# Rebuilt stage boundaries, another order in the RWKV core, and split operands in the mLSTM heads of a three-block network

## The chip, the cores and the metric

The program runs on one core of a Trainium2 chip. The core has five engines with a queue each: TensorE (PE; matmul, with its weight loads listed apart as PEld), VectorE (DVE), ScalarE (ACT), GpSimd (POOL), and SyncE (SP), which issues the DMAs. The metric is the device time of one execution in microseconds (us), lower is better. Times are medians over runs; the trace comes from one profiled execution.

## The reference

One sequence of 512 tokens, width 1024, float32 throughout, goes through three blocks, one layer each in the parts named here:

```python
# block 1: conv branch + sparse attention, merged; gelu FFN (2816) with a 3-tap conv; gated extra input; rmsnorm
# block 2: hyena mixer + FFN, then an RWKV-7 mixer (16 heads of 64, both directions) + FFN, rmsnorm
def step(state, inp):                      # RWKV-7, once forward and once backward, 512 steps
    sa = jnp.einsum('bhvk,bhk->bhv', state, kk_t)
    state = state * w_t[:, :, None, :] - sa[..., None] * (kk_t * a_t)[:, :, None, :] + v_t[..., None] * k_t[:, :, None, :]
    return state, jnp.einsum('bhvk,bhk->bhv', state, r_t)
# block 3: mLSTM (4 heads of 512) and HGRN2 (8 heads of 128) side by side, gated sum,
#          layernorm(ALPHA * x + mixed @ w_out), silu FFN, layernorm
w = jnp.exp(log_w - m_t[..., None]) * jnp.einsum('bhtd,bhsd->bhts', qc, kc)     # mLSTM
num, den = jnp.einsum('bhts,bhsd->bhtd', w, vc), jnp.sum(w, axis=-1)            # + carried state
h = num / jnp.maximum(jnp.abs(den), jnp.exp(-m_t))[..., None]
```

## The kernel before

Activations lie with channels on the 128 partitions and the 512 tokens along the free axis: eight tiles `x[0..7]` of 128x512. A dense layer (`dense`, `dense_steps`) takes chunks of 256 output channels. A chunk's weights arrive as `wraw` (1 MB by one DMA from SP); ACT rounds them to `wh` (line 156, reduced-precision fp32r), DVE takes the rest as `wl` (line 157), and the activations are split in the same way into `h` and `l`. `mm3` then adds `h*wh + l*wh + h*wl` in PSUM, three fp32r matmuls in place of one f32 matmul. A plain f32 matmul shows as two records in the trace. Where a sum over channels is wanted, a f32 matmul with a matrix of ones (`spread`) puts it on all partitions; POOL adds up the tiles before it (`sqa`, `lna`).

A scheduler orders the instructions of each engine from the dependencies, except where `manual_schedule` keeps the written order on the engines named. PE is in written order in the attention, the hyena mixer, the RWKV core and HGRN.

*RWKV core* (`core`, 1600 to 2257 us): eight pairs of heads go through a pipeline of stages written as Python generators, one step per `next`. In period p: `C` runs the recurrence over eight 64-token chunks of pair p-1 (three steps each: `R` is copied out of PSUM by DVE, `ch<-R,WT` follows, the new values `SV` are written by DVE for one head and by ACT for the other, then `ch<-SV,bkT`); `A`, `T`, `B` prepare pair p (`A`: gram products `pa/pb<-AX,bk`, which DVE multiplies by masks into `GB` (line 1419) and ACT copies into `AX` (line 1421); `T`: transposes `pb<-csts,bk` (line 1441); `B`: inverse of a triangular matrix, whose small part is solved on DVE row by row (`tw`, `W`) and comes back through DRAM and ACT as `wd`); `L`, `E` and `D` prepare pair p+1; `Y` ends pair p-2; `F` is one step of filling dense work (`pf<-x,wf`). `PLACES` gives each step a place, `ORDER` sorts them, and `FIRST` is the order of period 0:

```python
ORDER = [n for _, n in sorted((x, n) for n, v in PLACES.items() for x in v)]
for p in range(9):
    ...
    for n in ORDER if p else FIRST:
        if n in G:
            next(G[n], 0)
```

Only PE's order is fixed so; DVE, ACT and POOL are ordered by the scheduler.

*mLSTM* (`mlstm`, 2625 to 3092 us): per head, dense q, k, v and output gate, a lower-triangular weight matrix `pt` in four row blocks of 512, 384, 256 and 128 columns, and f32 matmuls of `pt` with ones (`pd`, the denominator) and with `v` (`po`), of constant rows (`rows`), and of two sums over channels. *HGRN* (`hgrn`, to 3345 us) weaves two heads and a stream of dense work step by step (`weave`). *LayerNorm* (class of that name, twice in block 3) sums six tiles, takes a preliminary mean off every tile (`center`), sums the squares (`lnq`, `lna`), corrects by the leftover mean `dm` (five tiles on DVE, three on POOL, line 1777), and scales and biases (lines 1782, 1783).

Of the kernel before, what the change touches and what calls it, by code (L numbers as in the profile page):

```python
# [83 lines left out]
class K:  # L84
# [179 lines left out]
    def begin(s):  # L264

        x, w = [], None
# [952 lines left out]
def key_norms(s, pairs, q, rid, ps, w):  # L1219
# [42 lines left out]
def core(s, ep, hw, ha, hg, xmd, xd):  # L1262
# [278 lines left out]
    def stage_c(p):  # L1541
# [6 lines left out]
        for i in range(8):  # L1548
# [16 lines left out]
            nc.scalar.activation(SV[HX[1], :, i, 1], q[HX[1], 1], AF.Copy, scale=-1.0)  # L1565
# [110 lines left out]
    def run(rp, pp):  # L1676
        env.rp, env.pp = rp, pp
        with s.tc.manual_schedule(engines={mybir.EngineType.PE}):
# [47 lines left out]
TAIL = 64  # L1726

# [677 lines left out]
```

## Time and profile before

| | us |
|---|---|
| time, median of 3 runs (lowest to highest) | 4038.02 (4033.47 to 4039.93) |
| the profiled execution: time | 4039.87 |
| the profiled execution: span in the trace | 4038.1 |
| busy PE / DVE / ACT / POOL | 3805.7 / 2391.3 / 1609.4 / 721.8 |
| mean granted TensorE clock | 0.967 |

The span runs from the first to the last instruction of the trace; 1.8 us of the execution lie around it. Busy times of different engines overlap. The granted clock is a share of 2.4 GHz; a stretch at 0.50 runs at 1.2 GHz.

### The profile page before, as it was taken

The page shows a single profiled execution, that of the slowest core. Times are in us where ns is not written, and L with a number is a line of the kernel's source. Part 1 is how long each engine was busy: PE and PEld are TensorE (multiplying, and loading weights), DVE is VectorE, ACT ScalarE, POOL GpSimd, SP SyncE. Part 2 cuts the span into 40 slices and gives each one's busy share as a digit, 9 for nine tenths or more (in the row PEclk, how much of TensorE's full clock was granted, in tenths as well). Part 3 has the DMA queues.
Part 4 walks back from the last instruction along what each step waited for, and adds up shares of the span by engine and source line. Part 5 has one row for each costly group of instructions (what it writes and reads, how often), then busy time and mean ns, then how long its engine had stood idle before and what let it go on. Part 6 is the DMA issues. An engine that isn't in the chain of part 4 may idle for free.

```text
span 4038.1 us, 51960 instructions
## 1 busy us (share of the span) xinstructions
PE 3805.7 (94%) x20982; PEld 2972.4 (74%) x20982; DVE 2391.3 (59%) x3492; ACT 1609.4 (40%) x2182; POOL 721.8 (18%) x574
## 2 busy tenths in 40 slices
PE   8899999999899998899878899999999999998998
PEld 6556888777788884666656688877777888877886
DVE  5965665677866556476675655465554644554334
ACT  3455433464443333344432433355553332333222
POOL 1000200032620006444442100101111000030001
PEclk9899999999999999999888999999999999999999
DMA  5122223222232324544433223132223212431221
GB/s 214 49 77 95 104 80 114 91 94 94 86 124 82 112 81 154 149 113 122 115 98 103 94 89 105 58 145 84 86 97 114 94 71 79 138 123 71 99 88 64
DMA packets 184132, 408.69 MB, mean 101 GB/s; under 512 B 80361, under 2 KB 98314, under 8 KB 155988
## 3 DMA queue, kind: packets, MB, share of 16 engines
q1 hardware_dynamic: 183892, 405.38, 30.3%
q8 instruction: 165, 2.70, 0.3%
q14 instruction: 75, 0.61, 0.0%
HBM read 364.37 MB, written 43.57 MB: 101 GB/s over the span
## 4 chain that ended last, share of the span: by engine, by line
PE 55%; DVE 9%; ACT 3%; DMA 2%; issue 2%; POOL 1%; SPq 0%; DVEq 0%; POOLq 0%; ACTq 0%
PE pacc L138 47%; PE pf L138 3%; PE pb L138 2%; PE ch L138 1%; PE pa L138 1%; DVE ct L1929 1%; DVE wl L157 1%; DVE tw L1471 1%; DVE GB L1419 1%; DVE W L1473 1%; PE py L138 1%; DMA x<-rid 0%; DVE xr L1151 0%; ACT wh L156 0%; DMA Lr<-dn 0%
## 5 line engine op out<-in xcount | busy, mean ns | idle before, releaser
L138 PE MATMUL pacc<-h,wh 128*128 128x512 f32 x3792 | 1499.7, 398 | 33.2 <-ACT wh L156 19.1
L138 PE MATMUL pacc<-l,wh 128*128 128x512 f32 x3792 | 1487.3, 392 | 1.2 <-DVE l L188 1.2
L138 PE MATMUL pacc<-h,wl 128*128 128x512 f32 x3792 | 1484.8, 393 | 3.8 <-DVE wl L157 3.8
L138 PEld LDWEIGHTS pacc<-h,wh 128*128 128x128 f32 x3792 | 718.7, 190 | 213.9 <-issue 30.8
L138 PEld LDWEIGHTS pacc<-h,wl 128*128 128x128 f32 x3792 | 716.8, 189 | 163.2 <-DVE wl L157 8.2
L138 PEld LDWEIGHTS pacc<-l,wh 128*128 128x128 f32 x3792 | 718.0, 189 | 151.7 <-issue 3.9
L157 DVE TENSOR_TENSOR wl<-wraw,wh 128x2048 fp32r<-128x2048 f32 (+2 forms) x276 | 611.4, 2215 | 368.2 <-ACT wh L156 368.0
L156 ACT ACTIVATE wh<-wraw 128x2048 fp32r<-128x2048 f32 (+2 forms) x276 | 492.8, 1785 | 790.3 <-PE pacc L138 694.0
L138 PE MATMUL pf<-x,wf 128*128 128x256 f32 x736 | 217.3, 418 | 5.6 <-DMA x<-yd 3.3
L223 POOL TENSOR_TENSOR sqa<-sq 128x512 f32<-128x512 f32 x12 | 19.3, 1608 | 1006.5 <-ACT sq L218 666.6
L138 PEld LDWEIGHTS pf<-x,wf 128*128 128x128 f32 x736 | 130.9, 197 | 39.5 <-issue 10.5
L295 DVE TENSOR_TENSOR z<-pacc,rstd 128x512 f32<-128x512 f32 x132 | 90.3, 691 | 101.5 <-PE pacc L138 101.2
L323 DVE TENSOR_TENSOR x<-pacc,x 128x512 f32<-128x512 f32 x48 | 33.1, 691 | 178.3 <-PE pacc L138 178.3
L223 POOL TENSOR_TENSOR sqa<-sqa,sq 128x512 f32<-128x512 f32 x50 | 100.3, 2006 | 109.3 <-ACT sq L218 101.2
L309 ACT ACTIVATE ct<-ct 128x512 f32<-128x512 f32 x66 | 41.8, 634 | 180.9 <-DVE ct L306 120.5
L138 PE MATMUL pacc<-wh,h 128*128 128x512 f32 (+2 forms) x288 | 103.6, 363 | 9.6 <-DVE z L983 9.6
L1836 POOL TENSOR_TENSOR x<-x,z 128x512 f32<-128x512 f32 x16 | 22.8, 1446 | 456.4 <-DVE z L1835 456.4
L138 PE MATMUL pacc<-wl,h 128*128 128x512 f32 (+2 forms) x288 | 103.4, 359 | 0.4 <-DVE wl L157 0.4
L138 PE MATMUL pacc<-wh,l 128*128 128x512 f32 (+2 forms) x288 | 103.1, 361 | 0.0
L290 DVE TENSOR_TENSOR hv<-ct,pacc 128x512 f32<-128x512 f32 x22 | 15.1, 688 | 143.6 <-PE pacc L138 143.6
L552 DVE SCALAR_TENSOR_TENSOR x<-sg,vecs,x 128x491 f32<-128x491 f32 (+28 forms) x120 | 86.2, 743 | 5.5 <-ACT x L543 5.0
L1422 POOL TENSOR_TENSOR AX<-AX,rwc 64x512 f32<-64x512 f32 x64 | 81.9, 1279 | 33.2 <-ACT AX L1421 29.6
(521 smaller groups left out, 4982.0 us busy)
## 6 DMA issues: line engine op xcount, KB each, us to landing
wraw<-in_w_up_dram SPq DMA_DIRECT2D x44, 1024.0 KB, 4.8
wraw<-in_w_down_dram SPq DMA_DIRECT2D x32, 704.0 KB, 4.0
wraw<-in_w_up2a_dram SPq DMA_DIRECT2D x22, 1024.0 KB, 4.8
wraw<-in_w_up2b_dram SPq DMA_DIRECT2D x22, 1024.0 KB, 4.8
x<-xmd SPq DMA_DIRECT2D x72, 256.0 KB, 2.7
wraw<-in_w1a_dram SPq DMA_DIRECT2D x16, 1024.0 KB, 4.8
wraw<-in_w3q_dram SPq DMA_DIRECT2D x16, 1024.0 KB, 4.9
wraw<-in_hy_w_in_dram SPq DMA_DIRECT2D x12, 1024.0 KB, 4.7
```

What stands on the lines that cost most here:

```text
L138: s.nc.tensor.matmul(out, a, b, start=start, stop=stop)
L156: s.nc.scalar.activation(wh[:, :n], raw[:, :n], AF.Copy)
L157: s.nc.vector.tensor_tensor(wl[:, :n], raw[:, :n], wh[:, :n].bitcast(F), op=SUB)
L223: nc.gpsimd.tensor_tensor(a2, acc, q, op=ADD)
L295: nc.vector.tensor_tensor(z, ps, rstd, op=MUL)
L309: nc.scalar.activation(t, t, act)
L552: nc.vector.scalar_tensor_tensor(y[:, d:], u[:, :T - d], w, y[:, d:], op0=MUL, op1=ADD)
L1419: nc.vector.tensor_tensor(GB[h, hs], q[h], mask[h, None].to_broadcast([64, 4, 2, 64]), op=MUL)
L1422: nc.gpsimd.tensor_tensor(AX[o, hs, X], AX[o, hs, X], mask[o, None].to_broadcast([64, 4, 2, 64]), op=MUL)
L1471: nc.vector.tensor_tensor(tw[:, 0:i, 0:i], W[:, 0:i, 0:i].rearrange("p j c -> p c j"), L[:, 0:i, i][:, None, :].to_broadcast([P, i, i]), o ...
L1473: nc.vector.tensor_reduce(W[:, i, 0:i], tw[:, 0:i, 0:i], axis=AX.X, op=ADD, negate=True)
L1929: nc.vector.scalar_tensor_tensor(t[:, d:], z[:, :T - d], w[3 - d], t[:, d:], op0=MUL, op1=ADD)
```

## The change

Three groups of edits are made together. At stage boundaries: `begin` loads `x` and the first weights in an interleaved order and splits those weights in four parts; a dummy activation (`ready`) loads ACT's table ahead of a norm; `phase(weights_last=True)` places the weight pool behind the activation pool in SBUF for the RWKV block's FFN and for block 3; the last `w_o` tile of the core lies in a `GB` buffer; LayerNorm's sums, shifts and scaling come in another order, written out by hand on PE, DVE and ACT, and its last step writes the split `h` and `l` directly; HGRN's sum of squares is made earlier and its matmul steps later. In the core: the `SV` copy of the second head goes from ACT to DVE, and `PLACES` and `FIRST` have other numbers. In the mLSTM heads: the f32 matmuls with `pt`, `v`, ones and rows become two or three fp32r matmuls with operands split by ACT and DVE (the block of 128 columns stays f32).

```diff
+    def parts(s, src):
+        h, l = (s.ap.tile([P, T], R, name="sp", tag="nrm", bufs=4) for _ in range(2))
+        s.nc.scalar.activation(h, src, AF.Copy)
+        s.nc.vector.tensor_tensor(l, src, h.bitcast(F), op=SUB)
+        return h, l
+    def mm2(s, out, w, hl, start, stop):
+        s.mm(out, w, hl[0], start, False)
+        s.mm(out, w, hl[1], False, stop)
+    def spread2(s, acc, onesr):
+        p = s.ms()
+        s.mm2(p, onesr, s.parts(acc), True, True)
+        return p
+    def ready(s, x):
+        t = s.ap.tile([P, 128], F, name="rdy", tag="rdy", bufs=1)[:, 0:1]
+        s.nc.scalar.activation(t, x[:, 0:1], AF.Abs_reciprocal_sqrt, scale=0.0, bias=s.eps(1.0))
     def sumsq_soon(s, xs):
         acc = s.sumsq_of(xs[:-1])
+        s.ready(xs[-2])
...
     def begin(s):
-        for n in range(NT):
-            if n == 2:
-                w = s.wsplit("w1a", 0, 8, 256)
-            x.append(s.xtile())
-            s.nc.sync.dma_start(x[n], s.I["xT"][n])
+        nc.scalar.activation(t, s.ones[:, 0:1], AF.Copy)
+        for i in range(4):
+            a = slice(512 * i, 512 * i + 512)
+            nc.sync.dma_start(x[2 * i], s.I["xT"][2 * i])
+            nc.sync.dma_start(raw[:, a], s.I["w1a"][0][:, a])
+            nc.sync.dma_start(x[2 * i + 1], s.I["xT"][2 * i + 1])
+            nc.scalar.activation(wh[:, a], raw[:, a], AF.Copy)
+            nc.vector.tensor_tensor(wl[:, a], raw[:, a], wh[:, a].bitcast(F), op=SUB)
...
 PLACES = {
-    "A": [1.21, 5.84, 5.85, 8.154, 8.47],
-    "T": [9.2, 10.47, 11.63, 11.63, 11.76, 11.76],
...
+    "A": [1.21, 5.84, 5.977, 6.971, 6.971],
+    "T": [10.229, 10.229, 10.402, 10.8, 11.732, 12.877],
...
             nc.vector.tensor_scalar(SV[HX[0], :, i, 0], q[HX[0], 1], -1.0, None, op0=MUL)
-            nc.scalar.activation(SV[HX[1], :, i, 1], q[HX[1], 1], AF.Copy, scale=-1.0)
+            nc.vector.tensor_scalar(SV[HX[1], :, i, 1], q[HX[1], 1], -1.0, None, op0=MUL)
...
-    def finish(s, g, b):
+    def finish(s, g, b, split=False):
...
         nc.scalar.activation(dm, s.p1, AF.Copy, scale=1.0 / 1024)
         nc.scalar.activation(w, s.p1, AF.Square, scale=1.0 / 1024)
+        for n in (4, 5, 6, 7, 0, 1):
+            shift(n)
+        nc.vector.scalar_tensor_tensor(w, s.p2, 1.0 / 1024, w, op0=MUL, op1=SUB)
+        nc.scalar.activation(r, w, AF.Abs_reciprocal_sqrt, bias=k.eps(1e-5))
+        nc.vector.tensor_scalar(v, w, 1.0, 1e-5, op0=MUL, op1=ADD)
+        shift(2)
...
             nc.vector.scalar_tensor_tensor(x, x, k.v(g, n), r, op0=MUL, op1=MUL)
+            if split:
+                out.append([k.ap.tile([P, T], R, name=i, tag="xs", bufs=16) for i in "hl"])
+                nc.scalar.activation(out[n][0], x, AF.Identity, bias=k.v(b, n))
+                if n:
+                    low(n - 1)
...
-        for c in range(4):
-            for i, _ in enumerate(s.dense_steps("w_out3", c, 8, 256, ms, evac_x, 2 * c)):
-                if (c, i) == (3, 2):
+        wo = s.wsplit("w_out3", 3, 8, 256)
+        w = s.wsplit("w_up3", 0, 8, 256)
+        with tc.manual_schedule(engines=MANUAL):
+            for i, _ in enumerate(s.dense_steps("w_out3", 3, 8, 256, ms, evac_x, 6, w=wo)):
+                if i == 2:
                     ln.mean()
-        ln.late(6)
-        ln.late(7)
-        ln.early()
-        ln.finish("ln1_g", "ln1_b")
+            s.ready(x[7])
+            ln.late(6)
+            ln.early()
+            ln.late(7)
+            xs = ln.finish("ln1_g", "ln1_b", split=True)
...
-    for si in range(4):
-        s.mm(pd[:, si * P:], s.ones, pt[:, off[si]:off[si] + T - si * P], si == 0, si == 3)
+    for si in range(3):
+        s.mm2(pd[:, si * P:], onesr, ps[si], si == 0, False)
+    s.mm(pd[:, 3 * P:], s.ones, pt[:, off[3]:], False, True)
...
-        for si in range(4):
-            s.mm(po[:, si * P:], v[:, si, j * P:(j + 1) * P], pt[:, off[si]:off[si] + T - si * P], si == 0, si == 3)
+        for si in range(3):
+            s.mm3(po[:, si * P:], vs[si][0][:, c], vs[si][1][:, c], *ps[si], si == 0, False)
+        s.mm(po[:, 3 * P:], v[:, c], pt[:, off[3]:], False, True)
...
-        yield
-        r = s.rstd_of(s.sumsq([o]), 1.0 / 128, 1e-6)
+        sq = s.sumsq_of([o])
+        yield
+        yield
+        yield
+        r = s.rstd_of(s.spread(sq), 1.0 / 128, 1e-6)
...
-            weave((head(2 * j), 22), (head(2 * j + 1), 22), (fill, (24, 40, 24, TAIL)[j]))
+            weave((head(2 * j), 24), (head(2 * j + 1), 24), (fill, (24, 40, 24, TAIL)[j]))
```

The order tables move instructions in rows, of which three places follow. Line numbers grow by 5 to 37 from before to after (1419 is 1456, 1349 is 1386, 1564 and 1565 are 1601 and 1602, 138 is 143).

On DVE, in the core's period 2 of the kernel before, around the masks of the second `A` pair (`GB`; the first line is the normalised key `x` of the next pair, which needs `rid`, a row of norms that comes back from DRAM):

```order
L1349 SCALAR_TENSOR_TENSOR x_13085<-x_13083,vecs_63,x_13085 128x512 [waits DMAHW5_49,DMAHW7_49,DMAHW3_49,DMAHW0_49]
L1419 TENSOR_TENSOR GB_13035<-pa_13036,rwc_10884 64x512 [waits PE_49]
L1419 TENSOR_TENSOR GB_13035<-pa_13037,rwc_10884 64x512 [waits PE_49]
L1419 TENSOR_TENSOR GB_13035<-pb_13052,rwc_10884 64x512 [waits PE_49]
L1419 TENSOR_TENSOR GB_13035<-pb_13053,rwc_10884 64x512 [waits PE_49]
L1555 COPY R_13076<-ch_13071 128x128 [waits PE_49]
L1564 TENSOR_SCALAR SV_12411<-ch_13071 64x2x64 [waits DVE_49,PE_49]
L1368 SCALAR_TENSOR_TENSOR e65_13367<-w65_13364,rwc_10884 128x520 [waits Activation_49]
```

And the same place in the changed kernel, from the third of the four masks on:

```order
L1456 TENSOR_TENSOR GB_13019<-pb_13036,rwc_10895 64x512 [waits PE_49]
L1456 TENSOR_TENSOR GB_13019<-pb_13037,rwc_10895 64x512 [waits PE_49]
L1601 TENSOR_SCALAR SV_12426<-ch_13006 64x2x64 [waits PE_49]
L1602 TENSOR_SCALAR SV_12426<-ch_13006 64x2x64
L1272 COPY fn_12825<-pa_13061 16x128 [waits PE_49]
L1612 TENSOR_TENSOR z1_13074<-ch_13006,Z_12960 128x128 [waits PE_49,Pool_49]
L1613 TENSOR_TENSOR SV_12426<-z1_13074,pcs_11770 64x2x64 [waits DVE_49]
L1614 TENSOR_TENSOR SV_12426<-z1_13074,pcs_11770 64x2x64
L1592 COPY R_13091<-ch_13086 128x128 [waits PE_49]
L1386 SCALAR_TENSOR_TENSOR x_13100<-x_13098,vecs_63,x_13100 128x512 [waits DMAHW6_49,DMAHW2_49,DMAHW0_49]
L1601 TENSOR_SCALAR SV_12426<-ch_13086 64x2x64 [waits DVE_49,PE_49]
L1602 TENSOR_SCALAR SV_12426<-ch_13086 64x2x64 [waits DVE_49]
```

The key that waits for a DMA stood ahead of the four masks, and now stands behind them, behind the new values `SV` of that chunk and behind the next `R`, directly ahead of the next two `SV`.

On PE, in period 2 before, from the second `A` pair to the first `T` (`pf` is a step of `F`; `ch` and `py` belong to `C`):

```order
L138 MATMUL pa<-AX,bk 128x128 x8
L138 MATMUL pb<-AX,bk 128x128 x8
L138 MATMUL pf<-x,wf 128x256
L138 MATMUL ch<-SV,AX 64x64 x4
L138 MATMUL py<-AX,SV 64x64 x4
L138 MATMUL pf<-x,wf 128x256
L1441 MATMUL pb<-csts,bk 128x64 x8
```

In the changed kernel the same stretch is longer; the piece begins behind the first `F` that follows the second `A` pair:

```order
L143 MATMUL ch<-R,WT 64x64 x4
L1270 MATMUL pa<-csts,fn 16x128
L143 MATMUL pf<-x,wf 128x256
L143 MATMUL ch<-SV,bkT 64x64 x4
L143 MATMUL py<-GB,SV 64x64 x4
L143 MATMUL pf<-x,wf 128x256 x2
L143 MATMUL ch<-SV,AX 64x64 x4
L143 MATMUL py<-AX,SV 64x64 x4
L143 MATMUL pf<-x,wf 128x256 x2
L143 MATMUL ch<-R,WT 64x64 x4
L143 MATMUL pf<-x,wf 128x256
L1478 MATMUL pb<-csts,bk 128x64 x16
```

Between the second `A` pair and the first `T` stood one step of `C` and two of `F`; now stand there four steps of `C`, seven of `F` and the row with `fn`.

On PE, at the first LayerNorm, the sums with the matrix of ones before (`x` are the last two tiles, `lnq` their squares, `lna` the sum of the other six squares):

```order
L138 MATMUL pacc_27002<-x_26756,ones_66 128x512 [waits DVE_49]
L138 MATMUL pacc_27002<-x_26758,ones_66 128x512 [waits DVE_49]
L138 MATMUL pacc_27003<-lnq_27036,ones_66 128x512 [waits Activation_49]
L138 MATMUL pacc_27003<-lnq_27040,ones_66 128x512 [waits Activation_49]
L138 MATMUL pacc_27003<-lna_27000,ones_66 128x512 [waits Pool_49]
```

and after:

```order
L143 MATMUL pacc_27300<-x_27046,ones_66 128x512 [waits DVE_49]
L143 MATMUL pacc_27301<-lnq_27334,ones_66 128x512 [waits Activation_49]
L143 MATMUL pacc_27301<-lna_27298,ones_66 128x512 [waits Pool_49]
L143 MATMUL pacc_27300<-x_27048,ones_66 128x512 [waits DVE_49]
L143 MATMUL pacc_27301<-lnq_27338,ones_66 128x512 [waits Activation_49]
L143 MATMUL pacc_27423<-h_27370,wh_27242 128x512 [waits Activation_49]
```

The sum of the six squares stood last and stands third; each tile's square follows its own tile; the last row is the first matmul of the FFN.

## Rows read from the trace of the kernel before

**Rows 1.** The page, first part: busy us, share of the span, instructions.

```profile
PE 3805.7 (94%) x20982; PEld 2972.4 (74%) x20982; DVE 2391.3 (59%) x3492; ACT 1609.4 (40%) x2182; POOL 721.8 (18%) x574
```

**Rows 2.** Windows by stage: us, busy of each engine, then PEclk, DMA share.

```profile
25.00:345.00 320.00, 292.75 (x1368) 198.47 (x1367) 229.00 (x534) 158.33 (x266) 19.50 (x15) 0.95 0.26 91
...
1690.00:1977.00 287.00, 263.24 (x3345) 188.92 (x3340) 194.19 (x433) 120.78 (x252) 133.51 (x142) 0.92 0.43 115
...
2625.00:3092.00 467.00, 462.05 (x1988) 360.28 (x1989) 259.17 (x281) 237.88 (x291) 63.11 (x51) 0.99 0.28 100
...
3620.00:3660.00 40.00, 21.66 (x52) 12.76 (x51) 31.62 (x36) 21.61 (x32) 14.68 (x8) 0.70 0.11 40
```

**Rows 3.** PE's waits in the core, 1600 to 2257 us: total, times, longest.

```profile
PE pa L138 <- DVE t L1382: 18.9, 7, 5.5
...
PE pb L1441 <- ACT AX L1421: 15.5, 5, 4.5
...
PE ch L138 <- DVE R L1555: 12.6, 17, 3.6
...
PE ch L138 <- ACT SV L1565: 7.2, 11, 1.3
...
PE pb L138 <- ACT wd L1498: 6.5, 2, 6.1
```

**Rows 4.** Windows at half clock, after a wait in the core and in HGRN.

```profile
1788.05:1798.25 10.20, 9.96 (x50) 6.21 (x50) 5.63 (x17) 5.55 (x9) 5.97 (x8) 0.50 0.40 80
...
3272.80:3276.30 3.50, 3.50 (x10) 2.70 (x9) 3.35 (x6) 2.60 (x3) 0.00 (x0) 0.51 0.16 62
```

**Rows 5.** Timeline of the start, ACT and POOL: start, us, what, idle before.

```profile
10.09 1.91 ACT L156 ACTIVATE wh<-wraw 128x2048 fp32r<-128x2048 f32 x1 [2.44 <-DMA wraw<-in_w1a_dram]
...
13.28 10.69 POOL L223 TENSOR_TENSOR sqa<-sqa,sq 128x512 f32<-128x512 f32 x6 [4.90 <-ACT sq L218]
```

**Rows 6.** Timeline of the core, DVE and PE.

```profile
1784.11 1.47 DVE L1349 SCALAR_TENSOR_TENSOR x<-x,vecs 128x512 f32<-128x512 f32 x1 [0.84 <-DMA x<-rid]
...
1785.50 1.40 DVE L1419 TENSOR_TENSOR GB<-pa,rwc 64x512 f32<-64x512 f32 x2
...
1788.29 1.11 PE L1441 MATMUL pb<-csts,bk 64*128 64x64 f32 x8 [2.23 <-ACT AX L1421]
...
1685.13 1.22 PE L138 MATMUL pa<-t,rwc 128*128 128x512 f32 x1 [5.52 <-DVE t L1382]
```

**Rows 7.** Groups by line, ACT in the core: busy, mean ns, idle before.

```profile
L1565 ACT ACTIVATE SV<-ch 64x128 f32<-64x128 f32 x64 | 17.4, 272 | 170.3 <-DVE SV L1564 170.1
```

**Rows 8.** Timeline of PE in the mLSTM stage, head 0.

```profile
2702.04 0.39 PE L138 MATMUL pacc<-wh,h 128*128 128x512 f32 x1
...
2702.27 0.39 PE L138 MATMUL pacc<-wl,h 128*128 128x512 f32 x1
...
2736.03 2.32 PE L138 MATMUL pacc<-pt,ones 128*128 128x512 f32 x8
...
2738.27 1.12 PE L138 MATMUL pacc<-rows,c 4*128 4x512 f32 x2
...
2739.32 8.90 PE L138 MATMUL pacc<-pt,v 128*128 128x512 f32 x32
```

**Rows 9.** PE's waits in the HGRN stage, 3092 to 3345 us.

```profile
PE pacc L138 <- ACT sq L218: 5.9, 3, 2.0
```

**Rows 10.** Timeline of the first LayerNorm, DVE, ACT and PE.

```profile
3636.48 6.30 DVE L1777 TENSOR_TENSOR x<-x,z 128x512 f32<-128x512 f32 x5 [2.80 <-ACT z L1774]
...
3647.08 1.38 ACT L1783 ACTIVATE x<-x,vecs 128x512 f32<-128x512 f32 x2 [2.27 <-DVE x L1782]
...
3649.03 1.22 PE L138 MATMUL pacc<-h,wh 128*128 128x512 f32 x2 [9.46 <-ACT h L187]
```

**Rows 11.** Timeline at the norm ahead of the RWKV mixer, ACT and PE.

```profile
1529.38 1.28 ACT L197 ACT_TABLE_LOAD   x1
...
1529.68 1.02 PE L138 MATMUL pacc<-sq,ones 128*128 128x512 f32 x2
```

More of the change, by code (lines that the diff above doesn't have):

```diff
@@ L1726 @@
 TAIL = 64
+MANUAL = {mybir.EngineType.PE, mybir.EngineType.DVE, mybir.EngineType.Activation}
 class LayerNorm:
@@ L1765, in late, with shift @@
         s.k.mm(s.p1, s.k.ones, s.x[n], n == 6, n == 7)
-        s.k.mm(s.p2, s.k.ones, s.last.pop(n), n == 6, False)
+        s.k.mm(s.p2, s.k.ones, s.last.pop(n), n == 6, n == 7)
     def early(s):
-        s.k.mm(s.p2, s.k.ones, s.q, False, True)
-    def finish(s, g, b):
+        s.k.mm(s.p2, s.k.ones, s.q, False, False)
+    def finish(s, g, b, split=False):
         k, nc = s.k, s.k.nc
-        dm, w = k.tmp("z"), k.tmp("ct")
+        dm, w, v, u = k.tmp("z"), k.tmp("ct"), k.tmp("ct"), k.tmp("ct")
+        r = k.ap.tile([P, T], F, name="rstd", tag="rstd", bufs=2)
+        def shift(n):
+            (nc.vector if n < 4 else nc.gpsimd).tensor_tensor(s.x[n], s.x[n], dm, op=SUB)
@@ L1786, in block3 @@
+        if split:
+            low(7)
+            for n, x in enumerate(s.x):
+                nc.scalar.activation(x, x, AF.Identity, bias=k.v(b, n))
+        return out
 def block3(s, x):
@@ L1797, in block3 @@
         ccol, rows = gates(s, x, bp)
+        onesr = bp.tile([P, P], R, name="onesr")
+        nc.scalar.activation(onesr, s.ones, AF.Copy)
+        selr = bp.tile([36, T], R, name="selr")
+        for a in (slice(0, 4), slice(32, 36)):
+            nc.scalar.activation(selr[a], cst[a, 0:T], AF.Copy)
+        cst = cst, onesr, selr
         for h in range(4):
-            mlstm(s, bp, h, xs, ccol, rows, cst, hA)
+            mlstm(s, bp, h, xs, ccol, rows, cst, hA, None if h else w)
     with tc.tile_pool(name="b3h", bufs=1) as bp:
@@ L1874, in during @@
                 ln.late(6)
-        s.ffn(x, xs, None, "w_up3", "w_down3", AF.Silu, update=upd, during=during)
+        s.ffn(x, xs, None, "w_up3", "w_down3", AF.Silu, update=upd, during=during, w=w)
+    with tc.manual_schedule(engines=MANUAL):
+        s.ready(x[7])
+        ln.early()
         ln.late(7)
-        ln.early()
-    ln.finish("ln2_g", "ln2_b")
+        ln.finish("ln2_g", "ln2_b")
     return x
@@ L1911, in gates, with mlstm, row @@
     nc.vector.tensor_copy(ccol, q)
-    return ccol, (mt, rows[32:36])
-def mlstm(s, bp, h, xs, ccol, rows, cst, hA):
+    hl = [bp.tile([36, T], R, name="rows" + i) for i in "hl"]
+    for a in (slice(0, 4), slice(32, 36)):
+        nc.scalar.activation(hl[0][a], rows[a], AF.Copy)
+        nc.vector.tensor_tensor(hl[1][a], rows[a], hl[0][a].bitcast(F), op=SUB)
+    return ccol, hl
+def mlstm(s, bp, h, xs, ccol, rows, cst, hA, w0):
     nc, I = s.nc, s.I
-    sel = cst[0:4, h * P:(h + 1) * P], cst[32:36, h * P:(h + 1) * P]
+    cst, onesr, selr = cst
     mneg = cst[:, 512:640]
+    def row(a):
+        p = s.ms()
+        a = slice(32 * a, 32 * a + 4)
+        s.mm2(p, selr[a, h * P:(h + 1) * P], [r[a] for r in rows], True, True)
+        return p
     qk = {}
@@ L1933, in mlstm @@
     for c in range(4):
-        s.dense("w3q", 4 * h + c, 8, 256, xs, evac_qk, 2 * c)
-    pn = s.ms()
-    s.mm(pn, sel[0], rows[0])
+        s.dense("w3q", 4 * h + c, 8, 256, xs, evac_qk, 2 * c, w=None if c else w0)
+    pn = row(0)
     nm = s.tmp("z")
@@ L2004, in mlstm @@
         acc = a
-    pm = s.ms()
-    s.mm(pm, s.ones, acc)
+    pm = s.spread2(acc, onesr)
     mu = s.tmp("z")
@@ L2381, in body @@
         x = block2b(s, x)
-        with s.phase():
+        with s.phase(weights_last=True):
             x = block3(s, x)
```

88 lines of the change are left out of this document (55 added, 33 removed), and 16 rows, old and new, of the table PLACES.

## The prediction

> **What bounds the kernel now.** I read the busy shares first: PE is busy 94% of the span, no other engine above 59% [rows 1]. So a stage either streams matmuls, and only fewer or cheaper matmuls shorten it, or PE waits, and then the wait that ends last counts. The windows by stage tell the two apart [rows 2]: the mLSTM stage has PE busy 462 of 467 us (matmuls bound it), the RWKV core from 1690 to 1977 us has 263 of 287 at a clock of 0.92, the first LayerNorm boundary 22 of 40 at 0.70, the attention 293 of 320. Then the waits of the two worst places were followed to what releases them.
>
> In the core PE's waits go to four causes of 7 us and more [rows 3]. The clock makes them dearer: behind the wait that ends at 1788.29 PE works 10.2 us at 0.50, half of 2.4 GHz, though it is busy 9.96 of them [rows 4]. The rule I take from these rows: behind a wait of some 2 us comes a stretch at half clock, and where PE is busy in it, half of it is lost. At 0.92 over 287 us, 0.08 x 287 / 0.5 = 46 us of the four full periods are at half clock.
>
> **The start.** Before, the first weights (1 MB in one piece) are rounded at 10.09, after ACT idled 2.44 us for that DMA, and POOL's chain of squares pauses 4.90 us, because ACT is at the weights when it should square the third tile [rows 5]. That chain sets the end of the first norm (13.28 + 10.69 = 23.97). With the weights in quarters and the table loaded early, squares come one after another, and the pause goes: -4.7 us. Bounds: -3 if ACT's four small roundings stay in its way, -6 if the load before the first tile counts too.
>
> **The core.** DVE runs strictly in order in this trace: at 1784.11 it stands 0.84 us for the DMA of `rid`, computes the key 1.47 us, and only then masks the second `A` pair into `GB` (four of 0.70 us). ACT's copy `AX` follows, and PE's first `T`, which needs that PSUM buffer, waits 2.23 us [rows 6]. Five such waits make 15.5 us [rows 3]. In the new order the key stands behind the masks, and seven `F` and four `C` lie between `A` and `T`, against four masks of 2.8 us in all. So the 15.5 us should go. Of the 46 us at half clock I give these waits 32 (four others, of 3.5 as behind HGRN's wait [rows 4], belong to `pa<-t,rwc`); half of it is lost, and a little more behind the fifth wait, in a later period: -17. In period 0, `E` moves behind thirteen `B` steps, and its wait of 5.52 us [rows 6] goes with some 3.5 us of lost clock (half of a stretch between the 3.5 and the 10.2 us of [rows 4]): -9. That is -41 at most.
>
> Against it: the second `SV` costs DVE 64 x 0.28 = 18 us (it was 17.4 on ACT [rows 7]), 2.3 us in a period; DVE is busy 194 of 287 us there, and 203 of a shorter time after. Before, ACT's `SV` started only after DVE's, so the pair is ready at the same moment as before; the waits on ACT's `SV` (7.2 us) turn into waits on DVE. What stays: `t` (18.9 less 5.5 us, since `E`'s own steps keep their neighbours), `R` (12.6 us over 17 times) and `wd`; a faster PE comes earlier to them, and the last `B` steps now follow one another with no `F` between. I take about two thirds, -26 us. Bounds: -41, and 0 if the recurrence takes all of it back.
>
> **The mLSTM heads.** The fp32r matmul of 512 columns starts every 0.227 us (2702.27 less 2702.04 [rows 8]); the f32 sums `pt,ones` over 512 + 384 + 256 + 128 columns take 2.24 us up to the next group, 0.90 for each 512 columns. Per head:
> - `pd`: two parts of 1152 columns are 2 x 2.25 x 0.227 = 1.02, and 0.25 for the f32 block: 1.27 against 2.24, -1.0.
> - two `rows`: 1.05 each (2739.32 less 2738.27) against 0.45: -1.2.
> - two sums over channels: 0.90 against 0.45: -0.9.
> - `po`: four times (3 x 0.51 + 0.25) = 7.1 against 8.9 with its tail, some 8.6 without: -1.5.
>
> Together -4.6 a head, -18.4 for four. Added are eight splits a head, each about 0.6 us on ACT and 0.7 on DVE, at engines busy 238 and 259 of 467 us [rows 2]; the six of `pt` and `v` lie under the dense matmuls of the output gate, the two of the sums lie on a path of their own, with PE meanwhile in the next head's dense work. If that cover is gone, in the last head, it is 1.3 us twice. I take -17.5, with bounds -19 and -10.
>
> **HGRN.** Three waits for ACT's square sum to 5.9 us [rows 9], two of them followed by 3.5 us at 0.51 with PE busy throughout [rows 4]: 5.9 + 2 x 1.7 = 9.3. The square now is issued two steps earlier and its matmul stands behind other work. I take -8, bounds -9.3 and -4.
>
> **The first LayerNorm.** Before, five shifts on DVE take 6.30 us ahead of the variance, and ACT does two bias adds (1.38) before the first `h` [rows 10]. After, two shifts (2.5) stand ahead of the variance, a third lies under ACT's root, and `h` is written with the bias: 3.8 + 1.4, less 0.4 for the shift that may stick out, -4.8. The preliminary mean moves from behind step 5 to behind step 3 of a chunk whose step has six matmuls: 2 x 6 x 0.227 = 2.7 earlier for all that follows. Sum -7.5 (bounds -4 and -10); PE's wait of 9.46 us ahead of the FFN stays a wait, of about half. The second LayerNorm has the shorter chain (-3.8), but its sum of `x` stands one f32 matmul (0.9) later, and one shift (1.3) stands inside the scaling: -1.6 (0 to -3).
>
> **What I cost at nothing.** The attention's PE order is the same; DVE and ACT there are reordered by the scheduler: 0, bounds -4 and +4 of 27 us of idle time [rows 2]. The restart behind the core still waits for the last `w_o` matmul, the DMA and the rounding. The early table load (`ready`) ahead of two norms: the load ends at 1530.66, the sum it precedes at 1530.70 [rows 11], so it is hidden by that matmul already, and 0.04 us is gained.
>
> The Trainium skill (ScalarE: Activation LUTs, section What ACT_TABLE_LOAD costs) puts a switch at about 1.28 us for the load and 1.38 for a drain, 2.66 in all. By that the two norms would gain some 1.3 us each, 2.7 together, and my sum would be 2.7 lower. The trace has the 1.28, and shows no drain beside it: the square ahead of the load ends as the load begins.
>
> **Sum.** -4.7 - 26 - 17.5 - 8 - 7.5 - 1.6 = -65.3. From the profiled execution's 4039.9 us that is 3974.6; the median of the runs is 1.9 lower: **3973 us**, rounded.
>
> **Rivals.**
> 1. *The core gives nothing back* (0.19): the wait moves. The key that waits for `rid` now stands directly ahead of the next two `SV`, and if the DMA is late, the recurrence's next matmul waits in place of `T`, with the same clock behind it. For it speak the 0.84 us that DVE stood for this DMA, and DVE's rising share; against it, that it stands some three steps of `C` later. Time 3973 + 26 = 3999.
> 2. *mLSTM gains nothing* (0.10): the splits delay the hand-over between heads, PE waits for what it saves. Against it stands ACT's and DVE's half-empty time. 3973 + 17.5 = 3990.
> 3. *Slower* (0.06): `wd` comes late to the first long `B` step. Its chain on DVE (`tw`, `W`) gets the 2.3 us of `SV` a period and the scans beside it, and its wait is already 6.1 us once [rows 3]. Without the core the rest gives -39.3, so the core would have to lose 47, 5.9 us in each of eight periods: a wait of 4.2 us and 1.7 of clock. From there it decides; time 4046.
> 4. *The early table load pays at the norms* (0.03): it is not hidden after all, and a whole load of 1.28 us goes at each of two norms [rows 11], 2.6 in all: 3970. The page of the Trainium skill named above points the same way.
>
> My own case (0.62) has 3946 to 3995. With the other cases the range is **3946 to 4010**: all bounds at their good end give 3946, the core at nothing and half of the other terms lost about 4010. A difference under 0.2% (8 us) can't be told from none in this kernel: faster 0.91, same 0.03, slower 0.06.
>
> **What would show it.** In the changed trace: no PE wait of over 1 us on `AX` in the core, and a clock above 0.95 in the four full periods; waits on `t` of 1.8 us still there; PE's `sq` waits gone in HGRN; about 4.4 us less for each mLSTM head with no new wait at the hand-over; the first matmul well before ACT's rounding at 10 us; PE's restart behind the LayerNorm some 8 us after the shifts start (12.6 before [rows 10]). Wrong it would be if `SV` or `wd` on DVE take over PE's waits in the core, or if the attention's new order on DVE loses more than 4 us.

## The result and the profile after

The changed kernel takes 3993.93 us (median of four runs, 3991.46 to 3994.21) where the kernel before takes 4036.18 beside it: a ratio of 0.9894, 95% interval 0.9879 to 0.9908. Run again later beside other kernels it took 3986.60 against 4038.24, 0.9872 (0.9857 to 0.9887). So the gain is 42 to 52 us; forecast were 65 from the profiled execution, with a range of 3946 to 4010. The profiled execution takes 3994.01 us, its span is 3992.2.

The page of the changed kernel, first part, answers to [rows 1] (busy us, share, instructions):

```profile
PE 3780.2 (95%) x21030; PEld 2970.0 (74%) x21030; DVE 2439.1 (61%) x3591; ACT 1605.3 (40%) x2157; POOL 736.4 (18%) x576
```

Windows of the same four stages answer to [rows 2] (us, busy of each engine, PEclk, DMA):

```profile
25.00:342.00 317.00, 291.00 (x1359) 197.44 (x1357) 226.54 (x531) 157.25 (x265) 17.60 (x15) 0.94 0.27 92
1688.00:1972.00 284.00, 259.22 (x3362) 188.22 (x3358) 212.98 (x482) 113.92 (x221) 136.30 (x145) 0.98 0.46 123
2602.00:3066.00 464.00, 456.04 (x2068) 369.67 (x2067) 292.60 (x313) 249.45 (x322) 78.35 (x52) 0.99 0.29 102
3586.00:3617.00 31.00, 19.56 (x56) 12.60 (x55) 27.77 (x32) 15.84 (x23) 12.73 (x8) 0.78 0.09 34
```

In the core PE's share of busy time is about the same (92 and 91%), but the clock rose from 0.92 to 0.98. DVE is busier by 19 us; the second `SV` is 10.0 of them (34 times 0.295 us), the rest is other work that falls into this window. PE's waits of the core, 1560 to 2270 us (total, times, longest), answer to [rows 3]:

```profile
PE ch L143 <- DVE SV L1602: 17.7, 19, 1.6
PE pa L143 <- DVE t L1419: 16.9, 6, 8.5
PE pacc L143 <- POOL sqa L228: 8.8, 1, 8.8
PE ch L143 <- DVE SV L1613: 6.8, 11, 1.3
PE ch L143 <- DVE SV L1614: 5.9, 7, 1.4
...
PE pb L143 <- ACT wd L1535: 3.8, 3, 2.9
...
PE ch L143 <- DVE R L1592: 3.5, 7, 1.7
```

The wait on `AX` is gone from the list. The one on `sqa`, the sum of squares behind the core, stands where the restart waited 6.8 us for ACT's rounding before; it belongs to the next stage. The waits of the recurrence (`SV`, `R`) are now 17.7 + 6.8 + 5.9 + 3.5 = 34 us on DVE; the same kinds were 12.6 and 7.2 [rows 3], with 4.9 on DVE's two later `SV` lines, so 25:

```profile
PE ch L138 <- DVE SV L1576: 4.0, 6, 1.8
PE ch L138 <- DVE SV L1577: 0.9, 1, 0.9
```

Starts of the same PE instruction in both traces show where the time came from:

| place | before | after | difference so far |
|---|---|---|---|
| first matmul that reads `pcs` (end of the start) | 99.30 | 96.85 | -2.5 |
| first matmul that reads `yy` of the last pair (end of the core) | 2241.14 | 2218.53 | -22.6 |
| `x,wif`, ahead of the mLSTM heads | 2630.14 | 2606.39 | -23.8 |
| first `h,wh` behind the first LayerNorm | 3649.03 | 3606.12 | -42.9 |
| end of the span | 4038.1 | 3992.2 | -45.9 |

Windows of the core alone, from the same matmul `hw,wl` to that `yy`, before and after (columns as above):

```profile
1577.60:2241.10 663.50, 572.43 (x6605) 403.03 (x6605) 413.90 (x889) 252.08 (x514) 292.62 (x299) 0.91 0.42 115
1575.33:2218.50 643.17, 563.86 (x6605) 399.31 (x6605) 435.14 (x951) 234.62 (x450) 296.17 (x299) 0.93 0.43 118
```

PE idles 91 us there before and 79 after, and is busy 8.6 us less with the same 6605 matmuls.

The core's step is not one number. Eight profiled executions have its new part unedited (the changed kernel twice, and the runs below that edit another stage or take this part alone). From `pcs` to `yy`, of which 1478 us lie ahead of the core, they need 2114.3 to 2123.9 us, mean 2119.6, against 2141.8 in the one of before, so -22.3 on average and -18 to -28 singly. The stages behind repeat far better: from `x,wif` to the first FFN matmul the two executions of the changed kernel need 999.73 and 999.65.

### The profile page after: what moved, and what is told of

Its sections match the earlier page's. It is cut to its first block, busy times and chain, and to the rows that moved or that the text cites. A ratio compares the mean times of both kernels' runs of the same rounds, so it can differ in the third digit from the quotient of the medians.

```text
span 3992.2 us, 52146 instructions
## 1 busy us (share of the span) xinstructions
PE 3780.2 (95%) x21030; PEld 2970.0 (74%) x21030; DVE 2439.1 (61%) x3591; ACT 1605.3 (40%) x2157; POOL 736.4 (18%) x576
## 4 chain that ended last, share of the span: by engine, by line
PE 76%; DVE 12%; ACT 4%; issue 3%; POOL 2%; DMA 2%; SPq 0%; DVEq 0%; ACTq 0%; POOLq 0%
PE pacc L143 68%; PE pf L143 3%; PE pb L143 2%; ACT wh L161 1%; PE ch L143 1%; DVE ct L2020 1%; DVE wl L162 1%; DVE x L589 1%; PE pa L143 1%; DVE tw L1508 1%; PE py L143 1%; DVE W L1510 1%; DVE GB L1456 0%; POOL sqa L228 0%; PE pacc L710 0%
## 5 line engine op out<-in xcount | busy, mean ns | idle before, releaser
L162 DVE TENSOR_TENSOR wl<-wraw,wh 128x2048 fp32r<-128x2048 f32 (+1 forms) x275 | 606.0, 2204 | 336.8 <-ACT wh L161 336.5
L161 ACT ACTIVATE wh<-wraw 128x2048 fp32r<-128x2048 f32 (+1 forms) x275 | 490.8, 1785 | 750.6 <-PE pacc L143 677.8
L228 POOL TENSOR_TENSOR sqa<-sqa,sq 128x512 f32<-128x512 f32 x50 | 91.8, 1835 | 110.3 <-ACT sq L223 102.2
L589 DVE SCALAR_TENSOR_TENSOR x<-sg,vecs,x 128x499 f32<-128x499 f32 (+28 forms) x120 | 86.1, 743 | 4.8 <-ACT x L580 4.4
L2020 DVE SCALAR_TENSOR_TENSOR ct<-z,vecs,ct 128x511 f32<-128x511 f32 (+2 forms) x96 | 86.7, 950 | 2.2 <-ACT ct L2018 1.9
```

Source lines behind the costliest of these rows:

```text
L161: s.nc.scalar.activation(wh[:, :n], raw[:, :n], AF.Copy)
L162: s.nc.vector.tensor_tensor(wl[:, :n], raw[:, :n], wh[:, :n].bitcast(F), op=SUB)
L228: nc.gpsimd.tensor_tensor(a2, acc, q, op=ADD)
L589: nc.vector.scalar_tensor_tensor(y[:, d:], u[:, :T - d], w, y[:, d:], op0=MUL, op1=ADD)
L2020: nc.vector.scalar_tensor_tensor(t[:, d:], z[:, :T - d], w[3 - d], t[:, d:], op0=MUL, op1=ADD)
```

## Experiments

**The core, in two halves.** The part on the core is a new table and one instruction moved. It was run whole, and each half alone (the table; the last two lines), on the kernel before.

```diff
-    "A": [1.21, 5.84, 5.85, 8.154, 8.47],
-    "T": [9.2, 10.47, 11.63, 11.63, 11.76, 11.76],
+    "A": [1.21, 5.84, 5.977, 6.971, 6.971],
+    "T": [10.229, 10.229, 10.402, 10.8, 11.732, 12.877],
...
-            nc.scalar.activation(SV[HX[1], :, i, 1], q[HX[1], 1], AF.Copy, scale=-1.0)
+            nc.vector.tensor_scalar(SV[HX[1], :, i, 1], q[HX[1], 1], -1.0, None, op0=MUL)
```

> The kernel before with the core's part of the change alone (new places, and the second SV on VectorE). Theory (the change's terms stand side by side): the two traces differ by 20.3 us over the core, so this gives -17 to -23 us, 4013 to 4019, with no wait of PE on AX over 1 us and a granted clock near 0.98 in the four full periods. Rival (the core's gain hangs on what the other parts did, or the landmarks put another stage's gain there): -12 us or less, 4024 or more.

> The kernel before, with only the second SV moved from ScalarE to VectorE; the places are the old ones. Theory (the order of the boundaries gives the gain, the move gives none): VectorE gets 18 us more ahead of the masks for GB, the AX waits of 15.5 us stay or grow, and ScalarE's SV waits of 7.2 us turn into VectorE's: 4034 to 4046. Rival (the move gives the gain, the places only follow it): -10 us or better, 4026 or less, with the AX waits smaller.

> The kernel before with the new places alone; the second SV stays on ScalarE. Theory (the order gives the gain, and VectorE's 18 us more of SV take part of it back): no AX waits over 1 us, clock near 0.98, waits on ScalarE's SV of some 7 us as before, VectorE's waits for SV and R under the 34 us seen after: -20 to -30 us, 4006 to 4016, as fast as the core's part whole or faster. Rival (the move is needed, since without it the pair of SV ends later than the new places allow): -10 us or less, 4026 or more, with long waits on ScalarE's SV.

| | us | ratio | 95% interval |
|---|---|---|---|
| both | 4013.25 | 0.9934 | 0.9922 to 0.9947 |
| `SV` alone | 4047.36 | 1.0018 | 1.0008 to 1.0028 |
| order alone | 4038.04 | 1.0001 | 0.9990 to 1.0011 |
| before, beside them | 4038.42 | | |

By the ratios the two halves make +7 and 0, and together -27 (0.0066 of 4038). `SV` alone came 1.4 us above the range stated for it. So the core's gain stands by itself, as the theory of the first run had it, but my theory of the third, that the order gives it and `SV` only costs, is wrong, and its rival holds. PE's waits in the core of the order alone, then of `SV` alone:

```profile
PE ch L138 <- ACT SV L1565: 50.0, 22, 6.2
PE ch L138 <- DVE R L1555: 8.2, 12, 2.0
```

```profile
PE pa L138 <- DVE t L1382: 18.4, 7, 8.4
PE pb L1441 <- ACT AX L1421: 16.8, 5, 4.8
PE ch L138 <- DVE SV L1565: 13.7, 11, 2.7
PE pb L138 <- ACT wd L1498: 10.6, 4, 6.4
```

In the order alone `AX` is gone, and 50 us of waits on ACT's `SV` have come, 43 more than [rows 3] has. ACT's timeline of that kernel at one of the longest, and PE's row there (start, us, what, idle before and what ended it):

```profile
1807.20 0.58 ACT L1210 ACTIVATE ft<-pf 128x512 f32<-128x512 f32 x1
1813.46 3.61 ACT L1498 ACTIVATE wd<-cm,rwc 128x128 f32<-128x128 f32 x12 [5.67 <-DMA cm<-dw]
1817.09 0.27 ACT L1565 ACTIVATE SV<-ch 64x128 f32<-64x128 f32 x1
```

```profile
1817.41 0.70 PE L138 MATMUL ch<-SV,bkT 128*64 128x64 f32 x8 [5.94 <-ACT SV L1565]
```

ACT stands 5.67 us for a DMA that brings the inverted blocks back from DRAM, then does twelve `wd` copies, and only then the 0.27 us that PE waits for. DVE had begun its half of the pair at 1810.73.

**Is it that queue?** Two runs keep the new order with `SV` on ACT and move the `wd` copies. In the first they are a step of their own at place 14.1; the second puts them at 17.1 and ties them behind the `SV` last issued (the diff is of the second, against the order alone; `FIRST` gets one `B` more in both).

```diff
-    "B": [10.49, 19.19, 19.303, 19.874, 20.066, 21.414, 22.296, 22.398, 23.386, 23.386, 23.386, 23.386, 23.442,
+    "B": [10.49, 17.1, 19.19, 19.303, 19.874, 20.066, 21.414, 22.296, 22.398, 23.386, 23.386, 23.386, 23.386, 23.442,
...
+        yield
         for d in range(2):
             u = st[d]
...
-                for blk in range(4):
-                    nc.scalar.activation(wd[:, :, blk], cm, AF.Copy, scale=cc("blk", blk, blk + 1))
+                with s.tc.issue_after(env.sv.ins) if env.sv else ExitStack():
+                    for blk in range(4):
+                        nc.scalar.activation(wd[:, :, blk], cm, AF.Copy, scale=cc("blk", blk, blk + 1))
...
+            env.sv = nc.scalar.activation(SV[HX[1], :, i, 1], q[HX[1], 1], AF.Copy, scale=-1.0)
```

> The kernel before with the new places and the second SV on ScalarE, as in the run of the order alone, and one thing more: ScalarE's sixteen wd copies, which read a DMA, are a step of their own at place 14.1 and no longer at 10.49, so that four SV stand ahead of them. Theory (the order alone gained nothing because ScalarE stands at wd for its DMA, 38.2 us in all, with the recurrence's SV queued behind it): ScalarE's idle time at wd falls under 10 us, PE's waits on ScalarE's SV from 50 to under 25 us, the time to 4008 to 4022. Rival (ScalarE is too late with SV for its own work, whatever stands at the DMA): waits on SV of 40 us or more, 4030 or more.

It took 4035.32 against 4037.14 (0.9996, 0.9987 to 1.0005), with 48.6 us of waits on ACT's `SV`. The rival's number came, but the run decides nothing: only PE's order is written by hand in the core, ACT's is the scheduler's, and it still put twelve copies ahead of the `SV` at the longest waits (idle for the DMA 36.8 us).

> The kernel before with the new places and the second SV on ScalarE, and ScalarE's wd copies at place 17.1, queued behind the SV of the sixth chunk by an order given to the scheduler (at 14.1 the scheduler had left them ahead of it). Theory (the order alone gains nothing because that SV stands behind the copies, which wait for a DMA): the waits of 5 to 6 us on ScalarE's SV go, their sum falls from 50 to 10 to 25 us, PE may wait up to 2 us in a period on wd instead, and the time falls to 4008 to 4024. Rival (the wait for the DMA is not what holds SV; ScalarE's other work does, or the wait turns into one on wd of the same length): 4030 or more.

With the copies really behind, it took 4013.31 against 4038.24: 0.9938 (0.9925 to 0.9950), as fast as the whole core part. PE's waits on `SV` fell from 50.0 to 22.0 us, and ACT's idle time for that DMA, in the answer on the copies' line, from 38.2 (first line: the order alone) to 14.1, as much as before the change:

```profile
PE ch L138 <- ACT SV L1567: 22.0, 19, 2.5
```

```profile
  DMA cm<-dw: 38.2, 9
  DMA cm<-dw: 14.1, 9
```

So the cause is shown: in the new order the `SV` on ACT stands behind copies that wait for a DMA, and moving either out of the other's way gives the same 25 to 27 us. Either of the two can be the one that moves. In the changed kernel ACT still idles 31.9 us for that DMA, but no `SV` stands behind it there.

> The changed kernel with the second SV back on ScalarE and the wd copies as a step of their own at place 14.1. Theory (the move of SV to VectorE only served to take it from behind the wd copies, and cost VectorE 18 us on the recurrence's path): the waits on VectorE's SV and R, 34 us after, fall by 8 us or more, ScalarE's SV adds some 7 us as before: -10 to +2 us against the changed kernel. Rival (SV on VectorE is quicker for the recurrence in itself, since both halves come from one engine with no hand-over): +8 us or more.

This is the changed kernel with `SV` back on ACT and the copies at 14.1; since that place moves nothing, it is in effect the order alone inside the changed kernel: 4008.18 against 4037.14, 0.9932 (0.9919 to 0.9944), 15 to 24 us behind the changed kernel (0.9894 and 0.9872), with 47.0 us of waits on ACT's `SV`. My theory fell and its rival's number came, but not for the rival's reason: with the copies behind it, `SV` on ACT was as fast as on DVE (4013.31 and 4013.25).

**The mLSTM.** Gates and heads back in f32 (of that the diff shows `pd` alone), then only the two sums over channels (the last two lines, and the second sum alike).

```diff
-    for si in range(3):
-        s.mm2(pd[:, si * P:], onesr, ps[si], si == 0, False)
+    for si in range(4):
+        s.mm(pd[:, si * P:], s.ones, pt[:, off[si]:off[si] + T - si * P], si == 0, si == 3)
...
-    pm = s.spread2(acc, onesr)
+    pm = s.spread(acc)
```

> The changed kernel with the mLSTM's sums, rows and products back in f32, and nothing else undone. Theory (the splits are worth 2.33 us a head, as the two traces' head periods of 108.4 and 110.7 say, and the wait of 2.78 us at the hand-over to HGRN comes with the tail's splits): +6 to +10 us against the changed kernel, 4000 to 4004. Rival (the splits are worth the 4.4 us a head of the forecast, and something else in the changed kernel slowed the stage): +15 us or more, 4009 or more.

3999.63 against 4038.42: 0.9901 (0.9888 to 0.9915), which the runs can't tell from the changed kernel. The traces can, since this stage repeats: from `x,wif` to the FFN's first matmul 1006.8 us against 999.7. The splits are worth 7.1 us, not 17.5; a head goes from 110.71 us (in the kernel before, 2738.27 to 2848.99 on the rows' matmuls) to 108.38 (2713.72 to 2822.10).

> The changed kernel with the mLSTM's two sums over channels back to one f32 matmul each; pt, v and rows stay in parts. Theory (each sum's split costs its path what the cheaper matmuls gain: a wait of 1.07 us for ScalarE's part in three heads, and the wait of 2.78 us with its half clock at the hand-over to HGRN in the fourth): the sp waits go, PE gets 2 x 0.4 us a head more work, 3.3 us less wait and 2.78 plus some 1.7 us less at the hand-over: -8 + 3.2 = -5 to 0 against the changed kernel, the head period within 0.4 us of 108.4, no wait over 1 us before the first HGRN matmuls. Rival (the split is hidden and the shortfall lies in the rows' matmuls at 0.33 us in place of 0.227): the head period grows by 0.8 us, and the waits at the hand-over stay: +3 to +5 us.

3985.45 against 4037.14: 0.9872 (0.9855 to 0.9889); against the changed kernel's second run no difference. In the trace the stage takes 996.6 us, 3.1 less than with all parts. The changed kernel's rows, ACT and then PE, in the second head and at the hand-over to HGRN:

```profile
2749.91 1.91 ACT L161 ACTIVATE wh<-wraw 128x2048 fp32r<-128x2048 f32 x1
2751.72 0.67 ACT L2015 ACTIVATE z<-pacc,vecs 128x512 f32<-128x512 f32 x1
2752.28 0.81 ACT L2018 ACTIVATE ct<-z,vecs 128x512 f32<-128x512 f32 x1
2752.99 0.62 ACT L244 ACTIVATE sp<-sqa 128x512 fp32r<-128x512 f32 x1
```

```profile
2753.66 0.50 PE L143 MATMUL pacc<-sp,onesr 128*128 128x512 f32 x1 [1.07 <-ACT sp L244]
...
3079.98 0.80 PE L143 MATMUL pacc<-h,wh 128*128 128x512 f32 x1 [2.78 <-ACT hq L2143]
```

The split of the sum stands behind the next weights on ACT, and PE, whose order is fixed there, waits 1.07 us in three heads. With f32 sums those waits go, but 1.67 us on `h`, a split of activations on ACT, come in each of three heads, and the head takes 109.03: 0.65 longer. So both theories hold by half: in the heads the parts pay 0.65, and at the hand-over they lose what that run gains (the 2.78 us become 1.38, and no half clock follows).

**The two together.** Parts in heads 0 to 2, f32 in head 3; and with that, the high part copied by DVE (the last two lines).

```diff
-    pm = s.spread2(acc, onesr)
+    total = s.spread if h == 3 else lambda a: s.spread2(a, onesr)
+    pm = total(acc)
...
-        s.nc.scalar.activation(h, src, AF.Copy)
+        s.nc.vector.tensor_copy(h, src)
```

> The changed kernel with the mLSTM's sums over channels in parts in heads 0 to 2 and as one f32 matmul in head 3. Theory (in the last head the splits stand on the path to HGRN, in the others they pay 0.6 us a head): the wait of 2.78 us at the hand-over and its half clock go as in the run with all sums in f32, and the head period stays at 108.4: -4 to -6 us against the changed kernel, about 2 us under the run with all sums in f32. Rival (the gain of that run came from the heads, not from the hand-over): within 1.5 us of the changed kernel.

> As the run with the last head's sums in f32, and the high part of the other heads' sums is copied by VectorE in place of ScalarE. Theory (PE's wait of 1.07 us in three heads comes from ScalarE's queue, where the part stands behind 1.9 us of weights and two evacuations): the sp wait falls under 0.5 us in each, 1.5 to 3 us less in all. Rival (VectorE's queue is as full there): the wait stays at 1 us or more, now on VectorE, and the time is the same or longer.

> The changed kernel once more, unedited, beside the others on the same chip. Expected: the ratio measured at first, 0.9894, within 0.0015; the two kernels before it in this list are then compared with it directly.

3986.73 (0.9870, 0.9856 to 0.9883), 3990.18 (0.9877, 0.9864 to 0.9891), and the changed kernel 3986.60 (0.9872, 0.9857 to 0.9887), against 4038.24. The changed kernel is 0.0022 under its first ratio, where 0.0015 was expected. None of them is faster than the changed kernel by more than the runs can tell. In the trace the first needs 993.5 us from `x,wif` to the FFN, 6.1 less than the changed kernel, as the theory had it; but its core came out 8.5 us longer than that of the changed kernel's second execution, with the same code, and by the time the rival's number came. Such a spread of the core hides 6 us; whether the edit is a gain in the mean stays open. DVE's copies made the wait longer, 1.63 us in place of 1.07, as that run's rival had it.

**The start.** The first norm sums the first tile alone; seven squares on ACT and seven adds on POOL are left out.

```diff
-        return xs, s.rstd_of(s.sumsq(x), 1.0 / 1024, 1e-6)
+        return xs, s.rstd_of(s.sumsq(x[:1] if g == "norm_mix" else x), 1.0 / 1024, 1e-6)
```

> The changed kernel, whose first norm sums the squares of the first tile alone: seven squares on ScalarE and seven adds on GpSimd are left out. Theory (the start's term was too large because VectorE's splits beside GpSimd's chain take 1.7 us in place of 0.7, so that PE waits 2.9 us for the low parts and the first chunk of matmuls, not the sum, sets the end): the splits take 0.7 us each, the three waits on l go, and the matmul of the sum starts 2 to 3 us before 23.41. Rival (the splits are slow for another reason, the DMA or the weights' quarters): they stay at 1.7 us and the waits stay.

Timelines, first of the changed kernel (DVE, POOL, PE), then of this one (DVE, PE):

```profile
15.14 3.44 DVE L196 SCALAR_TENSOR_TENSOR l<-x,vecs,h 128x512 fp32r<-128x512 f32 x2
...
9.96 9.78 POOL L228 TENSOR_TENSOR sqa<-sqa,sq 128x512 f32<-128x512 f32 x6 [0.39 <-ACT sq L223]
...
16.95 0.50 PE L143 MATMUL pacc<-l,wh 128*128 128x512 f32 x1 [1.71 <-DVE l L196]
...
23.41 1.02 PE L143 MATMUL pacc<-sqa,ones 128*128 128x512 f32 x2
```

```profile
15.13 1.41 DVE L196 SCALAR_TENSOR_TENSOR l<-x,vecs,h 128x512 fp32r<-128x512 f32 x2
...
23.71 0.50 PE L143 MATMUL pacc<-h,wh 128*128 128x512 f32 x1 [1.32 <-ACT wh L161]
```

A split takes 1.72 us beside POOL's adds and 0.70 without them, and the waits on `l` go, as the theory said. The sum's matmul comes at 5.24 there, since it needs one tile. But PE then waits for the next weights instead, and `pcs` is at 97.61, no earlier than 96.85. So neither the sum nor the `l` waits alone set the end of the start. The kernel was run once, in 3988.85 us.

## Why the forecast came out right, and where it was off

The direction and the range held. Against the sum of -65.3 the traces show -45.9, and every term that was given a size came out smaller. One bound was added up wrongly: the core at nothing and half of the other terms lost make 4018, not 4010; the measured time lies inside both. Only the core, the mLSTM's parts and the squares of the start were run by themselves; the other terms are read from traces in which all parts stand together.

- **Start**, -4.7: measured -2.5. POOL's chain does end 4.2 us earlier (9.96 + 9.78 = 19.74, against 23.97 by [rows 5]), as forecast. The step that failed is that this chain sets the end. Its matmul stands behind the first chunk in PE's order, and that chunk was held 2.9 us by the `l` splits on DVE; before the change too it started only at 25.14, 1.2 us behind the chain's end. What does set the end once both are gone is, by the run above, the next weights.
- **Core**, -26: measured -22 on average. What should go went: the `AX` waits (15.5), `E`'s 5.5, and half clock, which falls from 126 us (the stretches at 0.50 that begin between 1560 and 2240 us, added up) to 97 on average. Half of the difference is some 15 us of work; the two executions of the changed kernel show 8.6 and 14.4 in PE's busy time (572.4, 563.9 and 558.0 us), less than the 20.5 (17 and 3.5) that the sum of -41 has for the clock. The rule behind it, half clock behind a wait of some 2 us, fits most waits of the core but not all others: at 3192.30 a wait of 1.96 us was followed by 1.00. Of what I set against it, `R` and `SV` took 9 us back, and a `t` wait of 5.2 us in a late period grew to 8.5; the `t` waits of 1.8 us stayed, as said. But the step on `SV` failed. I wrote that the pair is ready at the same moment as before and priced the move as a cost. In the old order it is one, 7 us alone; in the new order nothing is gained without it, since 50 us of waits come on ACT's `SV`. I had looked for what the moved instruction does to DVE, and not for what it stood behind on ACT. That -26 came near is in part luck: it was a guess of two thirds of a sum that knew nothing of this.

What DVE takes back comes of its own order. Its rows at one of the 1.3 us waits, and PE's:

```profile
1789.66 0.33 DVE L1508 TENSOR_TENSOR tw<-W,L 128x100 f32<-128x100 f32 x1
1790.02 0.26 DVE L1510 TENSOR_REDUCE W<-tw 128x10 f32<-128x100 f32 x1
1790.31 0.36 DVE L1508 TENSOR_TENSOR tw<-W,L 128x121 f32<-128x121 f32 x1
1790.59 0.28 DVE L1601 TENSOR_SCALAR SV<-ch 64x128 f32<-64x128 f32 x1
1790.88 0.29 DVE L1602 TENSOR_SCALAR SV<-ch 64x128 f32<-64x128 f32 x1
```

```profile
1791.23 0.45 PE L143 MATMUL ch<-SV,bkT 128*64 128x64 f32 x8 [1.31 <-DVE SV L1602]
```

`SV` stands behind the chain of `tw` and `W`, which was on DVE before as well. That a place ahead of it would take these waits away is argued and wasn't tried.

The other terms:

- **mLSTM**, -17.5: measured -7.1, the largest miss, and under its lower bound of -10. Per head -2.3 in place of -4.4. `pd` (2.24 by [rows 8], now 1.36) and `po` (8.65, now 7.26) came about as sized. The two `rows` did not: by the rows below, their parts start 0.34 and 0.32 us after one another, not 0.227, so 0.66 a row where 0.45 was priced. The two sums gain 0.4 each and lose 1.07 to the wait on `sp`. Together that is a gain of 2.8 a head; why it is 2.3 stays open. The step that failed is that the splits' own path is covered in heads 0 to 2, and that it costs 1.3 twice in the last: the `sp` wait of 1.07 us came in three heads, and in the last it was 2.78 us on ACT's `hq`, a result of HGRN's first dense work, with half clock (0.54 for 3.3 us) behind. Rival 2 had the mechanism at less than its full price.
- **HGRN**, -8: some -5. The f32 run and the kernel before differ by 12.1 us from `x,wif` to the FFN, of which the LayerNorm has 7.1. The three waits on `sq` [rows 9] are gone with their half clock; two of 0.74 on `hk` have come, where one of 0.4 was.
- **First LayerNorm**, -7.5: measured -7.1 from the last `w_out3` matmul to the restart. The restart comes 9.4 us behind the first shift (3606.12 less 3596.69, below; 12.6 by [rows 10]), not 8: the third shift takes 1.75 us on DVE beside POOL's, and the root's first step 1.74. The rest is the earlier mean. PE's wait is 9.24 us, not half of 9.46 as forecast; it begins earlier.
- **Nothing** was right for the attention and the early table load: from 99.30 and 96.85 the difference stays at -2.3 to -2.5 through the norm at 1529, so rival 4 did not come. The restart behind the core gave 1.1, and not as I had it: it no longer waits for the rounding, but for POOL's sum of squares.
- **The second LayerNorm**, -1.6: measured -0.4 from its first sum of `x` to the end, since the same two steps on DVE take 1.75 and 1.74 us there. The FFN ahead of it, which I had left out, gave 2.6: behind its restart half clock lasts 5.7 us in place of 9.5, and a wait of 1.2 on `l` is gone.

Rows of the rows' parts in the changed kernel, and of the first LayerNorm, DVE and PE:

```profile
2713.72 0.49 PE L143 MATMUL pacc<-rowsh,selr 4*128 4x512 f32 x1
2714.06 0.39 PE L143 MATMUL pacc<-rowsl,selr 4*128 4x512 f32 x1
2714.38 0.50 PE L143 MATMUL pacc<-h 128*128 128x512 f32 x1
```

```profile
3596.69 2.36 DVE L1816 TENSOR_TENSOR x<-x,z 128x512 f32<-128x512 f32 x2 [2.09 <-ACT z L1818]
3606.12 2.07 PE L143 MATMUL pacc<-h,wh 128*128 128x512 f32 x4 [9.24 <-ACT h L1840]
```

Rival 1's mechanism (a key that holds `SV`) shows in no row of weight: the key stood up to 4.4 us for its DMAs, but PE's wait on the `SV` behind it was 0.83. Nor does rival 3's (`wd`, now 3.8 us).

## To carry to other kernels

Before pricing an instruction that moves to another engine, list what it stands behind on the engine that it leaves, in the new order and not in the old: here a wait of 5.67 us for a DMA in ACT's queue, with twelve copies behind it, cost PE 5.94 us on a copy of 0.27. Of two parts of a change one can be worth nothing and the other cost 7 us, and both together gain 27, so run the parts alone and whole before saying which one paid. A cheaper matmul that needs its operand split pays in full only where the split's engine is free at that moment: here the waits were 1.07 us in three heads and, in the last, where no next head covers the split, 2.78.

## What the runs showed of the hardware

An f32 operation on DVE with two operands in SBUF took 0.70 to 0.75 us alone and 1.72 beside POOL's adds of 1.63 each, whose shortest was 1.28. Steps with one operand in SBUF took 0.68 and 0.78 beside the same POOL work (the first LayerNorm, 3598.97 and 3599.68). The Trainium skill (SBUF — State Buffer, section SBUF: two separate sides) calls the port pair that VectorE and GpSimd share an exclusive lock, held for a whole instruction. The trace agrees in that each slows the other, in the start and in the first LayerNorm; whether for the whole instruction no run here shows. Both of my sums there left this term out.

The same program's core moved by 7.4 us between two executions (`pcs` to `yy` 2121.7 and 2114.3), together with the time at half clock (105.8 and 85.3 us in the stretches that begin between 1560 and 2240 us), while the stages behind `x,wif` repeated within 0.1 us. A difference of a few us in the core is not to be read from one pair of traces.
